# PEER selection for head pairs, one-hot factors of 16 tokens, and the order of POOL's and SyncE's queues

## The chip, the cores and the metric

The kernel runs on one core of one Trainium2 chip. The metric is the device time of one execution in microseconds (us), the median of several runs. The core has five engines that work through queues of their own and wait for each other by semaphores: TensorE (PE; its weight loads are listed as PEld), VectorE (DVE), ScalarE (ACT), GpSimd (POOL) and SyncE (SP), which issues most of the DMAs.

## The reference

Two transformer blocks work on 512 tokens of width 1024. The first is an attention and convolution block with a feed-forward part; the second is a mixer and, as its last step, a mixture of 16384 small experts (PEER). Only this last step is touched:

```python
def peer(h, w_q, sub_keys, expert_u, expert_v):
    q = jnp.einsum('bsd,dq->bsq', h, w_q).reshape(b, s_len, PEER_HEADS, 2, PEER_HALF)
    scores = jnp.einsum('bshpc,hpnc->bshpn', q, sub_keys).astype(jnp.float32)
    top_s, top_i = lax.top_k(scores, PEER_TOPK)
    cand_s = (top_s[..., 0, :, None] + top_s[..., 1, None, :]).reshape(...)
    cand_i = (top_i[..., 0, :, None] * PEER_NKEYS + top_i[..., 1, None, :]).reshape(...)
    best_s, best_pos = lax.top_k(cand_s, PEER_TOPK)
    best_i = jnp.take_along_axis(cand_i, best_pos, axis=-1)
    gate = jax.nn.softmax(best_s, axis=-1)
    ...
        u = jnp.take(expert_u, ib, axis=0)
        act = jax.nn.gelu(jnp.einsum('td,tkd->tk', xb, u), approximate=False)
        vv = jnp.take(expert_v, ib, axis=0)
        return jnp.einsum('tk,tkd->td', (gb * act).astype(h.dtype), vv)
```

There are 8 heads, 128 keys on each of two sides, and 16 experts chosen per head and token, so 128 experts of 128 x 128 for each token.

## The kernel before

The first 1290 us are the first block and the mixer, and then comes `peer`. Of its 512 tokens 384 (`TD`) take a dense path: the activations of all 128 chunks of 128 experts are computed for all of these tokens, and multiplied by a matrix of gates that is zero where an expert was not chosen. The last 128 tokens take the row path: the rows of `expert_u` and `expert_v` that they need are gathered by POOL's indirect DMAs (`r_row`, line 1145), 128 of each, and summed on VectorE.

**Weights.** A load brings 128 x 2048 f32 numbers into `wraw` (SyncE's queue, two buffers). ACT casts them to the leading part `whi` (line 142). The rest, `wlo`, is made by VectorE in one instruction (line 144) or by POOL in four slices of 128 x 512 (line 148). Each product on PE is three matmuls: `whi` with the leading part of the input, `whi` with its rest, and `wlo` with its leading part (lines 153 to 155).

**ahead.** This generator computes the activations of the first 48 expert chunks (`NS`) ahead of time: 24 loads of `expert_u`, two chunks each, 24 matmuls of 128 x 384 a chunk into `pa`, in four steps a chunk, 192 steps in all. For its first 13 loads `wlo` comes from POOL, for the others from VectorE. At a chunk's end ACT applies the gelu (`ex_a`, line 109) and SyncE stores it to `act_dram` (line 1115). The steps are called from `select` (8 for each of heads 0 to 6 and 40 for head 7, `AH`) and from `spread` (16, `LAST`, are held back for after it), and they are what PE does beside the selection.

**select.** It runs over the 8 heads. PE makes the queries of the next head and the scores of this one with the keys (`pb`), ACT copies the scores to `tk_s`, and VectorE finds the 16 best of each side with their indices (`top16`, lines 1184 to 1189: `tk_v`, `tk_i`). POOL adds pairs of them to 112 candidates per token in two instructions (`tk_c`, line 1250). VectorE finds the 16 best of these and their positions (`pk_b`, `tk_p`). The positions are turned into the two key indices of each chosen expert: `ranks` (lines 1197 to 1204), and then for each side a cast (1258), a compare with 0 to 15 (1260), a product with the indices (1263) and a sum over 16 places (1264), into `pk_i` and `pk_j`. At the end VectorE and ACT make the softmax of `pk_b`.

**Between.** `row_places` makes the addresses `r_at` of the row path on VectorE. POOL then issues the first six gathers of `row_experts`, at the line `next(rows)`.

**spread.** It makes the gate matrix for the 384 tokens. For each of three blocks of 128 tokens PE transposes `pk_i`, `pk_j` and `pk_b` (line 1293, `pb<-cst,pk_i`), and ACT copies them to `oh_t` and `oh_g`. Then for each group of 8 tokens VectorE makes four one-hot factors of 128 x 1024 f16: `oh_i` and `oh_j` by comparison (1309, 1311), and `oh_h` and `oh_l`, the factor of `oh_j` with the leading part of the gate and with its rest (1313, 1315), in three buffers each. PE multiplies them, 16 matmuls a group, four tokens to a PSUM bank (`pc`, `pd`, `pb` in turn; lines 1321 and 1322), ACT scales each bank into `oh_s` (1324), and SyncE stores `oh_s` once per 32 tokens to `gate_dram` (1330). Steps of `ahead` lie between the banks.

**experts.** `x_rows` loads the eight `xc` tiles of the residual (1092), PE transposes them in 40 instructions (1100), and ACT copies the results to `y` (1101). Then for each chunk `ex_a` is loaded back (1368), the gates `ex_g` too (1377; for the first chunk in twelve pieces), VectorE multiplies them to `ex_w` (1379), ACT casts it to `hew` (1383), VectorE makes the rest (`lew`, 1384), and PE multiplies them with the chunk of `expert_v` into `pp` (1416, 1417, 1420).

The order on each engine comes from a scheduler that works on the program's order and on dependencies; a tile that takes over the memory of a pool closed before waits for the readers of the old tiles.

## Time and profile before

| what | us |
|---|---|
| median of three runs | 2579.02 |
| lowest and highest of them | 2578.01, 2582.98 |
| the profiled execution, its time | 2575.19 |
| its span in the trace | 2573.4 |
| PE busy | 2489.6 (97%) |
| DVE busy | 1898.0 (74%) |
| ACT busy | 1100.5 (43%) |
| POOL busy | 617.4 (24%) |

The profile is of one execution. Its times count from the start of the span. A row of the timeline gives the start of an instruction, how long it lasted, its engine, line and tiles, and in brackets how long the engine had been idle before it and what ended that idle time. A wait for several things is put down to the one that came last. The granted clock is the mean of TensorE's clock as a share of full speed. A matmul's duration is longer than its distance from the next, since matmuls are pipelined.

### The profile page before, as it was taken

What the parts mean: (1) busy time and instruction counts of PE and PEld (TensorE: products, weight loads), DVE (VectorE), ACT (ScalarE), POOL (GpSimd) and SP (SyncE); (2) the same over time, 40 slices, a digit from 0 to 9 for tenths busy, and PEclk for the clock granted to TensorE, in tenths of its full rate; (3) what the DMA queues carried; (4) which work ended last, traced back from release to release, by engine and by line L of the source; (5) the groups of instructions that cost most, each with busy time, mean ns of one, the idle gap of its engine ahead of it and who ended that gap; (6) DMA issues with size and microseconds to landing.
All of it is one profiled execution on the core that took longest, in us unless ns stands there. A gap on an engine that the chain in (4) does not pass through costs nothing.

```text
span 2573.4 us, 33226 instructions
## 1 busy us (share of the span) xinstructions
PE 2489.6 (97%) x12637; PEld 2118.3 (82%) x12637; DVE 1898.0 (74%) x3238; ACT 1100.5 (43%) x1479; POOL 617.4 (24%) x510
## 2 busy tenths in 40 slices
PE   8999999999999999999999979989999999999999
PEld 6887877877888878777788967868889999999998
DVE  5558777745555567887789989847767777888887
ACT  4226555633222247657643248733333333333332
POOL 0001110111001101101054420001135555555552
PEclk9999999999999999999999989989999999999999
DMA  5352222444444331134333357689879999999995
GB/s 194 128 203 95 101 86 99 170 150 142 161 164 147 131 119 67 58 105 142 131 121 109 119 183 275 266 274 348 298 262 328 326 332 328 328 333 331 331 332 192
DMA packets 172313, 515.04 MB, mean 200 GB/s; under 512 B 13396, under 2 KB 78308, under 8 KB 146296
## 3 DMA queue, kind: packets, MB, share of 16 engines
q1 hardware_dynamic: 133960, 376.52, 41.7%
q0 software_dynamic: 37040, 135.35, 14.6%
q8 instruction: 99, 1.62, 0.2%
q10 hardware_dynamic: 1152, 1.05, 0.1%
q14 instruction: 62, 0.51, 0.1%
HBM read 461.47 MB, written 51.38 MB: 199 GB/s over the span
## 4 chain that ended last, share of the span: by engine, by line
PE 76%; DVE 14%; ACT 5%; issue 2%; DMA 2%; POOL 1%; SPq 0%; DVEq 0%; ACTq 0%; POOLq 0%
PE pa L155 12%; PE pa L153 11%; PE pa L154 11%; PE pp L1417 7%; PE pp L1416 7%; PE pp L1420 7%; PE pu L153 4%; PE pu L155 4%; PE pu L154 4%; ACT whi L142 1%; DVE wlo L144 1%; DVE tk_rest L1187 1%; PE pb L588 1%; PE pc L608 1%; DMA mg_a<-g_dram 1%
## 5 line engine op out<-in xcount | busy, mean ns | idle before, releaser
L142 ACT CAST whi<-wraw 128x2048 fp32r<-128x2048 f32 x229 | 437.7, 1911 | 573.0 <-PE pa L154 295.7
L144 DVE TENSOR_TENSOR wlo<-wraw,whi 128x2048 fp32r<-128x2048 f32 x210 | 492.8, 2346 | 139.0 <-ACT whi L142 134.3
L155 PE MATMUL pa<-hh,wlo 128*128 128x512 f32 (+1 forms) x1360 | 521.8, 385 | 19.8 <-POOL wlo L148 17.2
L153 PE MATMUL pa<-hh,whi 128*128 128x512 f32 (+1 forms) x1360 | 526.4, 387 | 14.9 <-ACT hh L228 10.8
L154 PE MATMUL pa<-lh,whi 128*128 128x512 f32 (+1 forms) x1360 | 523.1, 385 | 0.0
L155 PEld LDWEIGHTS pa<-hh,wlo 128*128 128x128 f32 x1360 | 257.7, 190 | 65.0 <-POOL wlo L148 18.9
L153 PEld LDWEIGHTS pa<-hh,whi 128*128 128x128 f32 x1360 | 258.0, 190 | 61.9 <-ACT hh L228 11.3
L1416 PE MATMUL pp<-whi,hew 128*128 128x512 f32 x768 | 300.1, 392 | 6.4 <-ACT hew L1383 6.4
L1417 PE MATMUL pp<-wlo,hew 128*128 128x512 f32 x768 | 300.6, 392 | 1.6 <-DVE wlo L144 1.6
L1145 POOL DMA_INDIRECT r_row<-in_u_rows,r_at x128 | 186.0, 1453 | 479.5 <-DVE r_w L1166 447.3
L154 PEld LDWEIGHTS pa<-lh,whi 128*128 128x128 f32 x1360 | 258.0, 190 | 44.2 <-issue 6.5
L1420 PE MATMUL pp<-whi,lew 128*128 128x512 f32 x768 | 237.6, 391 | 0.0
L1145 POOL DMA_INDIRECT r_row<-in_expert_v,r_at x128 | 194.9, 1522 | 177.1 <-DVE r_big L1174 139.5
L153 PE MATMUL pu<-hh,whi 128*128 128x384 f32 x640 | 217.0, 339 | 0.0
L155 PE MATMUL pu<-hh,wlo 128*128 128x384 f32 x640 | 216.7, 339 | 0.0
L154 PE MATMUL pu<-lh,whi 128*128 128x384 f32 x640 | 216.3, 338 | 0.0
L1416 PEld LDWEIGHTS pp<-whi,hew 128*128 128x128 f32 x768 | 144.6, 188 | 35.7 <-ACT hew L1383 6.6
L1417 PEld LDWEIGHTS pp<-wlo,hew 128*128 128x128 f32 x768 | 144.4, 188 | 30.4 <-DVE wlo L144 2.5
L1420 PEld LDWEIGHTS pp<-whi,lew 128*128 128x128 f32 x768 | 144.5, 188 | 30.4
L1174 DVE SCALAR_TENSOR_TENSOR r_big<-r_row,r_w,r_big 128x1024 f32<-128x1024 f32 x127 | 162.9, 1283 | 3.0
L1383 ACT CAST hew<-ex_w 128x384 fp32r<-128x384 f32 x128 | 65.6, 513 | 228.3 <-DVE ex_w L1379 151.3
L1166 DVE CUSTOM_DVE_ANT_0 r_row<-r_row,r_big 128x1024 f32<-128x1024 f32 x128 | 151.4, 1220 | 0.0
(436 smaller groups left out, 4552.5 us busy)
## 6 DMA issues: line engine op xcount, KB each, us to landing
wraw<-in_expert_u SPq DMA_DIRECT2D x64, 1024.0 KB, 7.2
wraw<-in_expert_v SPq DMA_DIRECT2D x64, 1024.0 KB, 7.6
wraw<-in_w_in SPq DMA_DIRECT2D x37, 1024.0 KB, 4.8
ada_w<-in_w_ada SPq DMA_DIRECT2D x24, 1024.0 KB, 4.8
gate_dram<-oh_s SPq DMA_DIRECT2D x12, 2048.0 KB, 6.9
ex_g<-gate_dram SPq DMA_DIRECT2D x31, 768.0 KB, 9.9
wraw<-in_w_up SPq DMA_DIRECT2D x16, 1024.0 KB, 5.9
wraw<-in_w_down SPq DMA_DIRECT2D x16, 1024.0 KB, 4.8
```

The costliest lines, as they stand in the source:

```text
L142: nc.scalar.copy(hi, raw)
L144: nc.vector.tensor_sub(lo, raw, hi.bitcast(F32))
L153: mm(out, wh, xh, start=start, stop=False)
L154: mm(out, wh, xl, start=False, stop=False)
L155: return mm(out, wl, xh, start=False, stop=stop)
L1145: self.nc.gpsimd.indirect_dma_start(t, None, src, at)
L1166: later(nc.vector.tensor_tensor_reduce(row, row, h, 1.0, 0.0, op0=ALU.mult, op1=ALU.add, accum_out=w[:, k:k + 1]))
L1174: later(nc.vector.scalar_tensor_tensor(acc, row, w[:, k:k + 1], acc, op0=ALU.mult, op1=ALU.add))
L1383: nc.scalar.copy(hi, w)
L1416: mm(sums[b][half], hi, v[0][:, c, hc], start=n == 0, stop=False)
L1417: mm(sums[b][half], hi, v[1][:, c, hc], start=False, stop=False)
L1420: mm(sums[b][half], lo, v[0][:, c, hc], start=False, stop=n == P - 1)
```

## The change

- **Places.** `places` works for two heads at once, after the odd one. The ranks are 128 wide, and there is one compare and one product of 128 x 4096 f16. The sum over 16 is a tree: additions of 256 x 8, 256 x 4 and 256 x 2 elements in f16, and four small ones into `pk_i` and `pk_j`. The indices `tk_i` and positions `tk_p` of two heads lie in one tile each.
- **Candidates.** Those of heads 6 and 7 are added on VectorE, the others on POOL as before.
- **First gathers.** The first six gathers are no longer issued before `spread` but in it, ahead of its second block of 128 tokens.
- **Spread.** A group is 16 tokens (`G`), so the one-hot factors are 128 x 2048, with two buffers each. A group fills four PSUM banks. `oh_g` and `oh_w` have one buffer.
- **experts.** The pools of `ex_a`, `ex_g` and the others (`et`, `ew`) are opened before `x_rows`, so that the `xc` tiles no longer share their memory with them.

```diff
@@ -25,6 +25,7 @@
 TB = 32
+G = 16
 NS = 48
@@ -1073,8 +1074,7 @@
                 rows = self.row_experts(rp, gp, rows)
-                next(rows)
-                self.spread(kp, Ix, Jx, gate, g_dram, ahead)
+                self.spread(kp, Ix, Jx, gate, g_dram, ahead, rows)
                 for _ in ahead:
@@ -1191,18 +1191,42 @@
         nc = self.nc
-        p4 = tp.tile([P, 64], U32, name="tk_u4", bufs=2)
-        p2 = tp.tile([P, 64], U32, name="tk_u2", bufs=2)
-        c = pos.rearrange("p t r -> p (t r)")
+        n = 128
+        p4 = tp.tile([P, n], U32, name="tk_u4", bufs=1)
+        p2 = tp.tile([P, n], U32, name="tk_u2", bufs=1)
+        c = pos.rearrange("p h t r -> p (h t r)")
         nc.vector.tensor_single_scalar(p4, c, 4, op=ALU.logical_shift_right)
         nc.vector.tensor_single_scalar(p2, c, 2, op=ALU.logical_shift_right)
-        a = tp.tile([P, 64], F32, name="tk_ra", bufs=2)
-        b = tp.tile([P, 64], F32, name="tk_rb", bufs=2)
+        ab = tp.tile([P, 2, n], F32, name="tk_r", bufs=1)
+        a, b = ab[:, 0], ab[:, 1]
         nc.vector.scalar_tensor_tensor(a, p2, -12.0, p4, op0=ALU.add, op1=ALU.max)
...
         nc.vector.tensor_sub(b, c, b)
-        return a, b
+        return ab
+
+    def places(self, tp, idx, pos, iota, h, dsts):
+
+        nc = self.nc
+        idf = tp.tile([P, 2, 2, 4, 16], F16, name="tk_f", bufs=1)
+        nc.vector.tensor_copy(idf, idx)
+        pf = tp.tile([P, 256, 2], F16, name="tk_pf", bufs=1)
+        nc.vector.tensor_copy(pf, self.ranks(tp, pos).rearrange("p s r -> p (s r)").unsqueeze(2).to_broadcast([P, 256, 2]))
+        eq = tp.tile([P, 256, 16], F16, name="tk_e", bufs=1)
+        nc.vector.tensor_tensor(eq.rearrange("p r (a b) -> p r a b", b=2), pf.unsqueeze(2).to_broadcast([P, 256, 8, 2]),
+                                iota, op=ALU.is_equal)
+        e = eq.rearrange("p (s r) n -> p s r n", r=16)
+        idf = idf.rearrange("p s h t n -> p (s h t) n").unsqueeze(2).to_broadcast([P, 16, 16, 16])
+        nc.vector.tensor_mul(e, e, idf)
+        n = 8
+        while n > 1:
+            nc.vector.tensor_add(eq[:, :, 0:n], eq[:, :, 0:n], eq[:, :, n:2 * n])
+            n //= 2
+        e = eq.rearrange("p (s h t r) n -> p s h t r n", s=2, h=2, t=4)
+        for s, dst in enumerate(dsts):
+            d = dst[:, :, 16 * h:16 * h + 32].rearrange("p t (h r) -> p h t r", h=2)
+            for i in range(2):
+                nc.vector.tensor_add(d[:, i], e[:, s, i, :, :, 0], e[:, s, i, :, :, 1])

@@ -1213,7 +1237,7 @@
             nc.vector.tensor_copy(iota, self.iota[:, 0:16])
-            iota = iota.rearrange("p (a b) -> p a b", b=2).unsqueeze(1).to_broadcast([P, 64, 8, 2])
+            iota = iota.rearrange("p (a b) -> p a b", b=2).unsqueeze(1).to_broadcast([P, 256, 8, 2])
             keys = tp.tile([P, 16 * P], F32, name="keys")
@@ -1229,8 +1253,10 @@
                 vals = tp.tile([P, 4, 2, 16], F32, name="tk_v", bufs=2)
-                idx = tp.tile([P, 4, 2, 16], U32, name="tk_i", bufs=2)
-                pos = tp.tile([P, 4, 16], U32, name="tk_p", bufs=2)
+                if h % 2 == 0:
+                    idx2 = tp.tile([P, 2, 2, 4, 16], U32, name="tk_i", bufs=2)
+                    pos2 = tp.tile([P, 2, 4, 16], U32, name="tk_p", bufs=2)
+                idx, pos = idx2[:, :, h % 2], pos2[:, h % 2]
                 for half in range(2):
@@ -1241,27 +1267,18 @@
                         tb, p = 2 * half + i // 2, i % 2
-                        self.top16(tp, sc[:, i * P:(i + 1) * P], vals[:, tb, p, :], idx[:, tb, p, :], P)
+                        self.top16(tp, sc[:, i * P:(i + 1) * P], vals[:, tb, p, :], idx[:, p, tb, :], P)
                     steps(AH[h] // 4)
...
                     o = cand[:, :, at:at + (a1 - a0) * n].rearrange("p t (a b) -> p t a b", b=n)
-                    nc.gpsimd.tensor_add(o, vals[:, :, 0, a0:a1].unsqueeze(3).to_broadcast(s),
+                    (nc.gpsimd if h < 6 else nc.vector).tensor_add(o, vals[:, :, 0, a0:a1].unsqueeze(3).to_broadcast(s),
                                          vals[:, :, 1, 0:n].unsqueeze(2).to_broadcast(s))
...
                     self.top16(tp, cand[:, tb, :], best[:, tb, h, :], pos[:, tb, :], NC)
-                idf = tp.tile([P, 4, 2, 16], F16, name="tk_f", bufs=2)
-                nc.vector.tensor_copy(idf, idx)
-                for p, src, dst in zip(range(2), self.ranks(tp, pos), (Ix, Jx)):
-                    pf = tp.tile([P, 64, 2], F16, name="tk_pf", bufs=2)
-                    nc.vector.tensor_copy(pf, src.unsqueeze(2).to_broadcast([P, 64, 2]))
-                    eq = tp.tile([P, 64, 16], F16, name="tk_e", bufs=3)
-                    nc.vector.tensor_tensor(eq.rearrange("p r (a b) -> p r a b", b=2),
-                                            pf.unsqueeze(2).to_broadcast([P, 64, 8, 2]), iota, op=ALU.is_equal)
-                    e = eq.rearrange("p (t r) n -> p t r n", t=4)
-                    nc.vector.tensor_mul(e, e, idf[:, :, p, :].unsqueeze(2).to_broadcast([P, 4, 16, 16]))
-                    nc.vector.tensor_reduce(dst[:, :, 16 * h:16 * h + 16], e, axis=AX.X, op=ALU.add)
+                if h % 2:
+                    self.places(tp, idx2, pos2, iota, h - 1, (Ix, Jx))
                 steps(AH[h] - AH[h] // 4 * 2)
@@ -1284,10 +1301,12 @@
             nc.vector.tensor_copy(iota16, self.iota)
-            iota = two(iota16).unsqueeze(1).to_broadcast([P, 8, P // 2, 2])
+            iota = two(iota16).unsqueeze(1).to_broadcast([P, G, P // 2, 2])
             after = self.last
-            left, groups, nb = NS * 4 - sum(AH) - LAST, TD // 8, 0
+            left, nb = NS * 4 - sum(AH) - LAST, 0
             for tb in range((TD + P - 1) // P):
+                if tb == 1:
+                    next(fetch)
                 pt = self.psum("b", 2)
@@ -1295,25 +1314,25 @@
                 nc.scalar.copy(ij.rearrange("p a b c -> p (a b) c"), pt[:, :2 * P].unsqueeze(2).to_broadcast([P, 2 * P, 2]))
-                gs = tp.tile([P, P], F32, name="oh_g")
+                gs = tp.tile([P, P], F32, name="oh_g", bufs=1)
                 nc.scalar.activation(gs, pt[:, 2 * P:3 * P], AF.Copy, scale=2.0 ** 14)
-                gh = tp.tile([P, 2, P, 2], F16, name="oh_w")
+                gh = tp.tile([P, 2, P, 2], F16, name="oh_w", bufs=1)
                 gs = gs.unsqueeze(2).to_broadcast([P, P, 2])
...
                 nc.vector.tensor_sub(gh[:, 1], gs, gh[:, 0])
-                for t0 in range(0, min(P, TD - tb * P), 8):
+                for t0 in range(0, min(P, TD - tb * P), G):
                     if t0 % TB == 0:
                         stage = tp.tile([P, P, TB], F32, name="oh_s")
-                    bc = lambda t: t[:, t0:t0 + 8].unsqueeze(2).to_broadcast([P, 8, P // 2, 2])
-                    oi = tp.tile([P, 8, P], F16, name="oh_i", bufs=3)
+                    bc = lambda t: t[:, t0:t0 + G].unsqueeze(2).to_broadcast([P, G, P // 2, 2])
+                    oi = tp.tile([P, G, P], F16, name="oh_i", bufs=2)
                     nc.vector.tensor_tensor(rows(oi), iota, bc(ij[:, 0]), op=ALU.is_equal)
-                    oj = tp.tile([P, 8, P], F16, name="oh_j", bufs=3)
+                    oj = tp.tile([P, G, P], F16, name="oh_j", bufs=2)
                     nc.vector.tensor_tensor(rows(oj), iota, bc(ij[:, 1]), op=ALU.is_equal)
-                    oh = tp.tile([P, 8, P], F16, name="oh_h", bufs=3)
+                    oh = tp.tile([P, G, P], F16, name="oh_h", bufs=2)
                     nc.vector.tensor_mul(rows(oh), rows(oj), bc(gh[:, 0]))
-                    ol = tp.tile([P, 8, P], F16, name="oh_l", bufs=3)
+                    ol = tp.tile([P, G, P], F16, name="oh_l", bufs=2)
                     nc.vector.tensor_mul(rows(ol), rows(oj), bc(gh[:, 1]))
-                    for f in range(2):
+                    for f in range(G // 4):
                         pg = self.psum("cdb"[nb % 3])
@@ -1323,10 +1342,10 @@
                                              pg.rearrange("p (t i) -> p t i", t=4), AF.Copy, scale=2.0 ** -14)
-                        n = (tb * P + t0) // 8 * 2 + f
-                        for _ in range((n + 1) * left // (2 * groups) - n * left // (2 * groups)):
+                        n = (tb * P + t0) // 4 + f
+                        for _ in range((n + 1) * left // (TD // 4) - n * left // (TD // 4)):
                             next(ahead, None)
-                    if (t0 + 8) % TB == 0:
+                    if (t0 + G) % TB == 0:
                         nc.sync.dma_start(g_dram[(tb * P + t0) // TB], stage)
@@ -1350,10 +1369,10 @@
         yp = es.enter_context(self.pool("ey"))
+        tp = es.enter_context(self.pool("et", bufs=2))
+        wp = es.enter_context(self.pool("ew", bufs=LEAD + 2))
         xs = self.x_rows(yp, x_dram)
         self.xs, self.g2 = xs, xs[4]
-        tp = es.enter_context(self.pool("et", bufs=2))
-        wp = es.enter_context(self.pool("ew", bufs=LEAD + 2))
         nb = TD // P
```

**POOL's queue at the end of the selection.** Before (`wlo` are the slices for `ahead`, `tk_c` the candidates of heads 6 and 7, `r_row` the gathers of the row path):

```order
L148 TENSOR_TENSOR wlo<-wraw,whi 128x512 x8
L1250 TENSOR_TENSOR tk_c<-tk_v 128x4x48
L1250 TENSOR_TENSOR tk_c<-tk_v 128x4x64
L148 TENSOR_TENSOR wlo<-wraw,whi 128x512 x8
L1250 TENSOR_TENSOR tk_c<-tk_v 128x4x48
L1250 TENSOR_TENSOR tk_c<-tk_v 128x4x64
L148 TENSOR_TENSOR wlo<-wraw,whi 128x512 x5
L1145 DMA r_row<-in_u_rows,r_at 128x1024 x6
L148 TENSOR_TENSOR wlo<-wraw,whi 128x512 x3
```

After (the first two rows are the candidates of head 5):

```order
L1276 TENSOR_TENSOR tk_c<-tk_v 128x4x48
L1276 TENSOR_TENSOR tk_c<-tk_v 128x4x64
L149 TENSOR_TENSOR wlo<-wraw,whi 128x512 x24
L1145 DMA r_row<-in_u_rows,r_at 128x1024 x128
L1145 DMA r_row<-in_expert_v,r_at 128x1024 x128
```

The candidates of heads 6 and 7 are gone from this queue, and all 24 slices now stand ahead of the first gather.

**SyncE's queue from the end of the spread to the first expert chunk.** Before (`xc` are the residual tiles that are transposed, `act_dram` the stores of the last chunks of `ahead`, `ex_a` and `ex_g` the loads for the experts):

```order
L1115 DMA act_dram<-ex_a 128x384
L1092 DMA xc_15245<-x_dram 128x512
L1092 DMA xc_15247<-x_dram 128x512
L1092 DMA xc_15249<-x_dram 128x512
L1092 DMA xc_15251<-x_dram 128x512
L1092 DMA xc_15253<-x_dram 128x512
L1115 DMA act_dram<-ex_a 128x384
L1092 DMA xc_15255<-x_dram 128x512
L1368 DMA ex_a<-act_dram 128x384
L1377 DMA ex_g<-gate_dram 128x128 x12
L1368 DMA ex_a<-act_dram 128x384 x2
```

After:

```order
L1092 DMA xc_14953<-x_dram 128x512
L1092 DMA xc_14955<-x_dram 128x512
L1115 DMA act_dram<-ex_a 128x384
L1092 DMA xc_14957<-x_dram 128x512
L1092 DMA xc_14959<-x_dram 128x512
L1092 DMA xc_14961<-x_dram 128x512
L1387 DMA ex_a<-act_dram 128x384
L1396 DMA ex_g<-gate_dram 128x128
L1115 DMA act_dram<-ex_a 128x384
L1396 DMA ex_g<-gate_dram 128x128 x11
L1387 DMA ex_a<-act_dram 128x384 x2
```

The eight `xc` loads stand closer together, and the loads `ex_a` and `ex_g` around the last store; before, `ex_a` and the first `ex_g` carry a wait for PE, and after they carry none.

**VectorE's queue in the spread.** Before, the second to fourth group (`oh_i`, `oh_j`, `oh_h`, `oh_l` are the one-hot factors):

```order
L1309 TENSOR_TENSOR oh_i<-oh_n,oh_t 128x1024
L1313 TENSOR_TENSOR oh_h<-oh_j,oh_w 128x1024
L1315 TENSOR_TENSOR oh_l<-oh_j,oh_w 128x1024
L1311 TENSOR_TENSOR oh_j<-oh_n,oh_t 128x1024
L1309 TENSOR_TENSOR oh_i<-oh_n,oh_t 128x1024
L1313 TENSOR_TENSOR oh_h<-oh_j,oh_w 128x1024
L1315 TENSOR_TENSOR oh_l<-oh_j,oh_w 128x1024
L1311 TENSOR_TENSOR oh_j<-oh_n,oh_t 128x1024
```

After, from the first group on:

```order
L1328 TENSOR_TENSOR oh_i<-oh_n,oh_t 128x2048
L1321 CAST oh_w<-oh_g 128x256
L1330 TENSOR_TENSOR oh_j<-oh_n,oh_t 128x2048
L1322 TENSOR_TENSOR oh_w<-oh_g,oh_w 128x256
L1332 TENSOR_TENSOR oh_h<-oh_j,oh_w 128x2048
L1334 TENSOR_TENSOR oh_l<-oh_j,oh_w 128x2048
L1328 TENSOR_TENSOR oh_i<-oh_n,oh_t 128x2048
L1330 TENSOR_TENSOR oh_j<-oh_n,oh_t 128x2048
L1328 TENSOR_TENSOR oh_i<-oh_n,oh_t 128x2048
L1332 TENSOR_TENSOR oh_h<-oh_j,oh_w 128x2048
L1334 TENSOR_TENSOR oh_l<-oh_j,oh_w 128x2048
L1330 TENSOR_TENSOR oh_j<-oh_n,oh_t 128x2048 x2
```

Each row now covers 16 tokens, and the `oh_i` of the next group stands ahead of the `oh_h` of this one as it did, but in one of two buffers and not of three.

## Rows read from the trace of the kernel before

**Rows 1.** The page, part 4: share of the span of the chain that ended last.

```profile
PE 76%; DVE 14%; ACT 5%; issue 2%; DMA 2%; POOL 1%; SPq 0%; DVEq 0%; ACTq 0%; POOLq 0%
```

**Rows 2.** Waits of PE, whole span: what, total us, times, longest us.

```profile
PE pa L155 <- POOL wlo L148: 17.2, 3, 9.5
...
PE pp L1416 <- ACT hew L1383: 6.4, 1, 6.4
```

**Rows 3.** Slices: length, busy us of PE, PEld, DVE, ACT, POOL; granted clock; DMA share; GB/s.

```profile
1460.00:1470.00 10.00, 8.39 (x45) 7.33 (x44) 9.90 (x67) 3.33 (x5) 6.35 (x7) 1.00 0.00 1
...
1480.00:1490.00 10.00, 3.84 (x22) 3.51 (x20) 9.90 (x64) 2.67 (x3) 2.39 (x4) 0.86 0.05 19
1490.00:1500.00 10.00, 9.99 (x46) 9.96 (x47) 9.86 (x39) 0.24 (x1) 4.91 (x4) 0.80 0.51 152
1500.00:1510.00 10.00, 2.02 (x11) 1.42 (x9) 6.10 (x9) 6.58 (x8) 6.70 (x5) 0.88 0.56 191
1510.00:1520.00 10.00, 7.27 (x28) 7.18 (x29) 7.04 (x4) 2.48 (x4) 4.80 (x5) 0.61 1.02 396
```

**Rows 4.** Timeline of POOL, 1486 to 1503: start, us, instruction, idle before it.

```profile
1487.02 0.51 POOL L1250 TENSOR_TENSOR tk_c<-tk_v 128x192 f32<-128x192 f32 x1 [12.28 <-DVE tk_v L1188]
...
1488.70 6.21 POOL L148 TENSOR_TENSOR wlo<-wraw,whi 128x512 fp32r<-128x512 f32 x5
1502.09 3.01 POOL L1145 DMA_INDIRECT r_row<-in_u_rows,r_at  x1 [7.17 <-DVE oh_n L1286]
```

**Rows 5.** Timeline of PE, 1490 to 1513.

```profile
1490.01 0.69 PE L155 MATMUL pa<-hh,wlo 128*128 128x384 f32 x1 [6.18 <-POOL wlo L148]
...
1501.53 0.33 PE L1293 MATMUL pb<-cst,pk_j 128*128 128x128 f32 x1 [1.26 <-DVE pk_j L1264]
...
1512.73 0.69 PE L155 MATMUL pa<-hh,wlo 128*128 128x384 f32 x1 [9.45 <-POOL wlo L148]
```

**Rows 6.** Groups of VectorE, 1305 to 1502: busy us, mean ns, idle before.

```profile
L1263 DVE TENSOR_TENSOR tk_e<-tk_e,tk_f 128x1024 f16<-128x1024 f16 x16 | 13.8, 866 | 0.2
...
L1264 DVE TENSOR_REDUCE pk_j<-tk_e 128x64 f32<-128x1024 f16 x8 | 9.7, 1217 | 0.2
...
L1202 DVE TENSOR_SCALAR tk_rb<-tk_ra 128x64 f32<-128x64 f32 x8 | 5.3, 667 | 0.2
```

**Rows 7.** Timeline of VectorE, 1494.9 to 1496.

```profile
1494.99 0.68 DVE L1270 TENSOR_TENSOR pk_b<-pk_b,pk_t 128x512 f32<-128x512 f32 x1
...
1495.83 0.19 DVE L1202 TENSOR_SCALAR tk_rb<-tk_ra 128x64 f32<-128x64 f32 x1
```

**Rows 8.** Groups of all engines in the spread, 1519 to 1665.

```profile
L1324 ACT ACTIVATE oh_s<-pc 128x512 f32<-128x512 f32 x32 | 36.4, 1138 | 5.6 <-PE pc L1322 5.3 <-ACT oh_s L1324 0.3
...
L1309 DVE TENSOR_TENSOR oh_i<-oh_n,oh_t 128x1024 f16<-128x1024 f16 x48 | 32.8, 683 | 5.7 <-ACT oh_t L1297 3.1 <-PE pd L1322 2.1 <-PE pb L1322 0.5
...
L144 DVE TENSOR_TENSOR wlo<-wraw,whi 128x2048 fp32r<-128x2048 f32 x9 | 20.5, 2280 | 0.0
```

**Rows 9.** Stretches: spread, long products after it, start of experts, experts.

```profile
1524.40:1664.90 140.50, 129.97 (x1207) 112.65 (x1205) 132.25 (x197) 116.73 (x126) 0.00 (x0) 0.99 0.64 249
1664.90:1680.10 15.20, 15.20 (x89) 15.20 (x87) 2.29 (x1) 4.92 (x6) 0.00 (x0) 1.00 0.72 274
1680.10:1698.80 18.70, 9.27 (x42) 6.41 (x40) 0.56 (x1) 6.66 (x12) 0.00 (x0) 0.73 0.46 140
1720.00:2555.00 835.00, 834.96 (x4093) 746.73 (x4092) 657.51 (x722) 288.77 (x302) 370.01 (x247) 1.00 0.90 318
```

**Rows 10.** Timeline of SyncE at the start of the experts.

```profile
1690.71 5.54 SPq L1377 DMA_DIRECT2D ex_g<-gate_dram  x12
```

**Rows 11.** Timeline of VectorE there.

```profile
1697.70 0.56 DVE L1379 TENSOR_TENSOR ex_w<-ex_a,ex_g 128x384 f32<-128x384 f32 x1 [26.92 <-DMA ex_g<-gate_dram]
```

**Rows 12.** Timeline of PE there.

```profile
1686.40 4.70 PE L1100 MATMUL pu<-cst,xc 128*128 128x128 f32 x20 [0.25 <-ACT y L1101]
...
1698.86 0.80 PE L1416 MATMUL pp<-whi,hew 128*128 128x512 f32 x1 [6.38 <-ACT hew L1383]
```

More of the change, by code (lines that the diff above doesn't have):

```diff
@@ L1276, in select, with spread @@
         return Ix, Jx, gate.rearrange("p a h r -> p a (h r)")
-    def spread(self, kp, Ix, Jx, gate, g_dram, ahead):
+    def spread(self, kp, Ix, Jx, gate, g_dram, ahead, fetch):
         nc = self.nc
```

## Prediction

> **What bounds the kernel now.** I read the page first, then the waits of TensorE, then TensorE's busy time in slices of 10 us, then the instructions around the two slices that stand out. The chain that ended last lies 76% on PE [rows 1], so a microsecond counts when PE loses it. The reader should look for places where PE stops in the last part of the program (the selection, the spread and the start of the experts), since only that part is touched. The waits name them: 17.2 us in three waits for a `wlo` made on POOL and one wait of 6.4 us for `hew` [rows 2]. The slices put them in time: 8.39 us of work at 1460 to 1470, 3.84 at 1480 to 1490, 2.02 at 1500 to 1510, and 7.27 at 1510 to 1520 [rows 3].
>
> **Transition from selection to spread.** PE stops three times for the same reason: POOL works its queue in order, and what stands ahead of the next `wlo` waits for VectorE. Before the first product at 1490.01 PE was idle 6.18 us for `wlo` [rows 5]; POOL had itself waited 12.28 us for `tk_v` before the candidates at 1487.02 and only then, at 1488.70, took up the `wlo` [rows 4]. Before 1512.73 PE was idle 9.45 us [rows 5]; POOL had waited 7.17 us for `oh_n` and then issued six gathers from 1502.09 on, with the last three `wlo` slices behind them [rows 4]. The third wait of the 17.2 is what is left, 17.2 - 9.5 - 6.2 = 1.5 us, and lies in the slice at 1460 (10 - 8.39 = 1.6). Both long stops are followed by a stretch at the lower of the two clocks (1.2 against 2.4 GHz; the granted clock is 0.80 and 0.61 in the slices behind them [rows 3]). At full clock a product of this chain comes every 15.2 / 86 = 0.177 us (the stretch after the spread, where 86 long products, of the row's 89, run without a stop [rows 9]). The slice from 1490 spent 9.99 us on 46 products and the slice from 1510 7.27 us on 28 [rows 3], so the low clock cost 9.99 - 8.14 = 1.9 and 7.27 - 4.96 = 2.3 us. One more wait, 1.26 us for `pk_j` at 1501.53 [rows 5], belongs here.
>
> The change takes both obstacles out of POOL's queue: the candidates of heads 6 and 7 go to VectorE, and the gathers go behind all 24 slices. POOL then runs at PE's pace: one load of weights is four slices of 6.21 / 5 = 1.24 us [rows 4] and feeds 48 products of 8.5 us. So all of 1.6 + 6.2 + 1.9 + 1.3 + 9.5 + 2.3 = **22.8 us** can go, if VectorE is ready when PE comes. PE would reach the transposes of `pk_i` at 1501.5 - 1.3 - 1.6 - 6.2 - 1.9 = 1490.5.
>
> VectorE's side: per head the two one-hot compares, two products and two sums cost 2 x (0.87 + 0.87 + 1.22) = 5.9 us if a compare costs what a product does, with nine small instructions of up to 0.67 on top [rows 6], so about 18 us for two heads. For the pair I take one rate for all f16 work with two inputs. An f32 subtraction costs 0.68 us at 512 elements [rows 7] and 2.28 at 2048 [rows 8]; an f16 one of 1024 costs 0.68 [rows 8], as f32 of half the size. So f16 of 2048 should cost about 1.22 and of 4096 about 2.3. Compare 2.3, product 2.3, tree 1.2 + 0.7 + 0.4, four last adds 0.9, ranks and casts 2.3: 10 us; with the tree at f32's rate 12, with the small ones stretched as now up to 15. I take 12, so 6 us saved per pair. The candidates cost VectorE about 0.8 us a head (256 and 192 f32 elements). VectorE ends `pk_j` now at 1501.5; the last pair's places replace 9 us of head 6 and 9 of head 7 by 12 at the end, and the earlier pairs save too, so 1501.5 - 6 - 6 + 1.6 = 1491 if only one earlier pair's saving reaches the end, 1486 if more. That is level with PE's arrival; I take 22.5 of it and keep 0 to 5 us as a loss.
>
> Here the trace shows that VectorE and POOL disturb each other: the `tk_rb` operation costs 0.19 us by itself and 0.67 on average over the selection [rows 6, 7]. The Trainium skill ("SBUF — State Buffer", section "SBUF: two separate sides") says that VectorE's instructions in its two-port modes or with two inputs in SBUF and GpSimd's share a port pair under a lock held for a whole instruction, so that the later one waits. By that rule the new 2.3 us instructions would hold POOL up, and POOL's slices the small ones. The stretched row agrees with it; its price is the second rival below.
>
> **Spread.** Now 192 one-hot instructions of 0.68 us [rows 8] come every 0.6 us (132.25 us busy less 20.5 for nine `wlo` and some 3 for small ones, over 184 [rows 8, 9]): 115 us. After: 96 of 1.22, every 1.14: 109.5. VectorE is busy 132 of 140.5 us here and PE 130 [rows 9], and neither is alone the bound; ACT is busy 117. ACT's 96 evacuations of 1.14 us [rows 8] stay the same, and so do PE's 768 small products. What changes on PE is their grain: 32 at once, then 15 to 20 of the long ones, with three PSUM banks for four evacuations per group, and two buffers of 16 tokens instead of three of 8. In VectorE's order the `oh_i` of the next group stands before the `oh_h` and `oh_l` of this one, as it did, but it must now wait until PE has ended the group two before, not three. Working the steady order through by hand with these durations gives 5.4 us per 16 tokens where few long products lie between and 5.8 to 6.2 where many do; now it is 140.5 / 24 = 5.85. The six gathers inside cost nothing: POOL is idle for the whole spread [rows 9] and their data are used after it. From first one-hot product to the end of the long ones (155.7 us now, with 86 long products behind the last one-hot; 94 after) I take a gain of **2 us**; bounds: all of VectorE's 5.5 plus its idle time, 7, on one side, and 8 us lost on the other.
>
> **Start of the experts.** Now PE ends the long products at 1680.1 and starts the first expert product at 1698.86, 18.8 us later, at granted clock 0.73 [rows 9, 12]. `ex_a` and the twelve `ex_g` loads can't be issued before the transposes have read the `xc` tiles, since they lie in the same memory: they start at 1690.71 and take 5.54 us to issue; `ex_w` starts at 1697.70 and `hew` at once behind it [rows 10 to 12]. With their own memory they follow `act_dram` directly: the last store is issued after the last gelu, for which I allow 0.9 us, eleven loads take 11 x 0.46 = 5.1, and landing takes the same 1697.70 - (1690.71 + 5.54) = 1.45, so `ex_w` could start at end + 7.5. Then the 40 transposes with their 10 copies, which stay ahead of the first product on both engines, become the bound: 20 transposes now take 4.70 us [rows 12], so 40 take 9.4, and a last copy and `hew`, half a microsecond each, follow. First product at end + 10.4, gain 8.4. A low clock such as the one that cost 1.9 and 2.3 us above follows this wait too (the first product lasts 0.80 us [rows 12]) and may go or not. I take **9.5**, with half of it; bounds 7 to 11. Everything behind, 835 us in which PE never stops [rows 9], is untouched.
>
> **Sum.** 22.5 + 2 + 9.5 = 34. The profiled execution took 2575.2, so 2541; the runs' median is 2579.0, 3.8 above it, so **2545**. With the losses above (5, 10 and 2.5) and gains (0, 5 and 1.5) the forecast's own range is 2537 to 2553.
>
> **Rivals.**
> - *Coupled buffers.* With two buffers, VectorE and PE wait for each other in each group and the spread loses 8 to 12 us: 2555. For it: VectorE and PE both lie above 92% in the spread [rows 9], with no other slack. Against: only 24 hand-overs instead of 48.
> - *The wait changes its name.* VectorE is late with the last pair, since nine small instructions are stretched by 0.5 us each behind POOL (4.3 us), or the tree is slow: PE waits 4 to 9 us at `pk_i`, and may drop to the low clock: 2551 to 2554. This is what the lock of the Trainium skill ("SBUF — State Buffer", section "SBUF: two separate sides") would do; the stretched row speaks for it.
> - *VectorE alone bounds the spread*, and its whole saving arrives: 2538.
> - *Slower than before.* The cycle of a group becomes serial: four one-hot instructions 4.55, then 32 small products 1.8, then the last evacuation 0.9, 7.3 us per 16 tokens instead of 5.85. That costs 24 x 1.4 = 34 us and eats the whole gain; from 7.3 us per group it decides, and at 7.6 the time is 2586. For it: the two buffers. Against: VectorE's order starts the next group's `oh_i` and `oh_j` before the last is used.
> - *It does not do what it says.* Next in line behind POOL's `wlo` are the loads of `wraw` (two buffers) and ACT's casts, which may be late as well; with half the transition and a bad spread the net is near zero: 2575 to 2584.
>
> **How the numbers follow.** Forecast 0.56, coupled buffers 0.14, changed name 0.12, VectorE alone 0.08, slower 0.06, nothing 0.04. The range takes in the first four: 2534 to 2560, and leaves out about 0.18. This kernel's measurements tell 0.2%, 5 us, from no change. Faster 0.90, same 0.04, slower 0.06.
>
> **What would show it.** Right: no wait of PE for POOL's `wlo`, first one-hot product near 1502 (now 1524.4), spread of 138 to 141 us, first expert product 9 to 10.5 us after the long ones, `ex_g` issued before the transposes. Wrong: a wait of PE for `pk_i` or `pk_j` over 4 us, one-hot instructions of 2048 elements well over 1.25 us, PE waits for `oh_h` or `oh_i` that sum to over 10 us, or a low clock in the spread.

## The result and the profile after

The changed kernel takes 2547.05 us (median of four runs, 2545.76 to 2549.65) where the kernel before takes 2579.2. The ratio is 0.9874, with a 95% interval of 0.9857 to 0.9891. The forecast was 2545, with a range of 2534 to 2560. The profiled execution took 2545.76, with a span of 2544.0 (before 2573.4): 29.4 us less.

The waits of PE from the first one-hot product (1500.9) to the end of the long products (1660.9) are these (what, total us, times, longest us):

```profile
PE pd L1340 <- ACT oh_s L1343: 8.9, 15, 1.3
PE pc L1340 <- ACT oh_s L1343: 6.1, 14, 0.7
PE pa L154 <- ACT ex_a L110: 1.0, 1, 1.0
PE pb L1340 <- DVE oh_h L1332: 0.7, 1, 0.7
```

The wait for POOL's `wlo`, 17.2 us in [rows 2], is gone from the whole profile. The waits for `oh_s` are now 29, of 15.0 us: PE wants to write a PSUM bank that ACT has not scaled yet. Before there were six, of 5.7 us:

```profile
PE pd L1321 <- ACT oh_s L1324: 3.9, 4, 1.1
PE pc L1321 <- ACT oh_s L1324: 1.8, 2, 1.0
```

The slices over the old gaps, in the columns of [rows 3]:

```profile
1470.00:1480.00 10.00, 10.00 (x58) 10.00 (x57) 9.79 (x46) 2.87 (x4) 5.03 (x4) 1.00 0.49 154
1480.00:1490.00 10.00, 9.65 (x56) 9.20 (x55) 9.72 (x14) 4.31 (x4) 0.33 (x1) 1.00 0.35 136
1490.00:1500.00 10.00, 9.51 (x55) 9.19 (x54) 9.12 (x11) 6.51 (x9) 8.78 (x5) 1.00 0.73 256
```

In the slices from 1480 and 1490 PE works 9.65 and 9.51 us at a granted clock of 1.00; before, it worked 3.84 us in the first and ran at a granted clock of 0.80 in the second [rows 3]. POOL and PE at the transition (start, us, instruction, idle before):

```profile
1473.43 5.03 POOL L149 TENSOR_TENSOR wlo<-wraw,whi 128x512 fp32r<-128x512 f32 x4 [3.44 <-ACT whi L143]
1489.67 3.01 POOL L1145 DMA_INDIRECT r_row<-in_u_rows,r_at  x1 [11.21 <-DVE oh_n L1303]
```

```profile
1488.83 0.30 PE L1312 MATMUL pb<-cst,pk_i 128*128 128x128 f32 x1 [0.35 <-DVE pk_i L1229]
1500.88 0.23 PE L1340 MATMUL pc<-oh_i,oh_h 128*128 128x128 f16 x1
1669.83 0.50 PE L1435 MATMUL pp<-whi,hew 128*128 128x512 f32 x1 [1.41 <-ACT hew L1402]
1680.02 1.66 PE L1435 MATMUL pp<-whi,hew 128*128 128x512 f32 x6 [1.63 <-ACT whi L143]
```

POOL ends its last slice 11 us before the gathers, and PE waits 0.35 us for `pk_i`: VectorE and PE arrive together. The stretches of [rows 9], now spread, long products behind it, start of experts:

```profile
1500.90:1644.20 143.30, 126.46 (x1197) 114.65 (x1196) 127.24 (x106) 111.97 (x125) 0.69 (x1) 1.00 0.68 266
1644.20:1660.90 16.70, 16.70 (x99) 16.66 (x97) 2.29 (x1) 5.99 (x8) 0.00 (x0) 1.00 0.75 274
1660.90:1669.80 8.90, 6.16 (x41) 4.16 (x39) 0.60 (x2) 6.50 (x12) 0.00 (x0) 1.00 0.70 215
```

So the time went as follows:

| stage | before | after | gain | forecast |
|---|---|---|---|---|
| to the first one-hot product | 1524.4 | 1500.9 | 23.5 | 22.5 |
| from there to the end of the long products | 155.7 | 160.0 | -4.3 | 2 |
| from there to the first expert product | 18.7 | 8.95 | 9.8 | 9.5 |
| from there to the end | 874.5 | 874.2 | 0.3 | 0 |

Of the 23.5 us, 1.0 lies ahead of the selection, where nothing was changed: VectorE's first instruction of the selection, the copy `tk_n`, starts that much earlier in the profiled execution (before, then after):

```profile
1301.18 1.28 DVE L1215 CAST tk_n<-iota 128x16 f16<-128x16 f32 x1
1300.16 1.28 DVE L1239 CAST tk_n<-iota 128x16 f16<-128x16 f32 x1
```

From `tk_n` to the first one-hot product the selection took 223.2 us and now takes 200.7, which is 22.5 us less.

### The profile page after: what moved, and what is told of

Same layout as the page of the kernel before. It is cut to its first block, busy times and chain, and to the rows that moved or that the text cites. A ratio compares the mean times of both kernels' runs of the same rounds, so it can differ in the third digit from the quotient of the medians.

```text
span 2544.0 us, 33077 instructions
## 1 busy us (share of the span) xinstructions
PE 2478.2 (97%) x12637; PEld 2114.3 (83%) x12637; DVE 1868.4 (73%) x3094; ACT 1098.0 (43%) x1479; POOL 627.2 (25%) x506
## 5 line engine op out<-in xcount | busy, mean ns | idle before, releaser
L1145 POOL DMA_INDIRECT r_row<-in_u_rows,r_at x128 | 190.2, 1486 | 467.2 <-DVE r_w L1166 430.6
## 6 DMA issues: line engine op xcount, KB each, us to landing
ex_g<-gate_dram SPq DMA_DIRECT2D x31, 768.0 KB, 11.3
```

What stands on the lines that cost most here:

```text
L1145: self.nc.gpsimd.indirect_dma_start(t, None, src, at)
```

## Experiments

All runs change the changed kernel; medians of four runs. `tk_n` starts anywhere from 1300.1 to 1303.8 in these runs, though nothing ahead of it differs, and totals scatter by 2 to 3 us. So a stage is read from its own length, and the selection from `tk_n` on: 200.6 to 200.9 us in the runs that leave it alone (199.1 with groups of 8 in the scheduler's order).

### What each part is worth: one part undone

**The first gathers back before the spread.**

```diff
+                next(rows)
                 self.spread(kp, Ix, Jx, gate, g_dram, ahead, rows)
...
-                if tb == 1:
-                    next(fetch)
```

> The changed kernel with the first six gathers issued before the spread again. If they cost what the prediction took, the idle of 9.5 us and the low clock of 2.3 us behind it, the time is 2547 + 8 to 12 = 2555 to 2559, with a wait of TensorE for POOL's wlo of 7 to 10 us. If POOL, free of the candidates of heads 6 and 7, has made all its slices before the gathers come up, nothing changes: 2546 to 2549.

2548.74 us, no wait of PE for POOL's `wlo`; selection and spread as in the changed kernel (200.9 and 160.1 us). POOL had ended its slices at 1480.0 and had nothing else to do when the gathers came up, 11.3 us later. The gathers' move is worth nothing beside the other parts. The run doesn't bring back the old queue, though: no slice stands behind the gathers here, where three did before, so what that order would cost beside the faster places was not tried.

**Candidates of heads 6 and 7 back on POOL.**

```diff
-                    (nc.gpsimd if h < 6 else nc.vector).tensor_add(o, ...
+                    nc.gpsimd.tensor_add(o, ...
```

> The changed kernel with the candidates of heads 6 and 7 back on POOL. The run with the gathers moved back showed that these cost nothing by themselves, so by elimination the candidates should be what freed POOL: then TensorE's waits for POOL's wlo come back (1.6 and 6.2 us and 1.9 at the low clock), 2554 to 2558. Rival: with the faster places VectorE delivers tk_v early enough, POOL is held up by less than the lead it has, and the time is 2546 to 2550; then it was the places that removed the waits.

2551.99 us, 4.9 more, by neither mechanism as I had put it: POOL's `wlo` isn't waited for, although POOL waits for `tk_v` again. POOL's timeline, and PE's one new wait:

```profile
1470.70 0.51 POOL L1276 TENSOR_TENSOR tk_c<-tk_v 128x192 f32<-128x192 f32 x1 [2.93 <-DVE tk_v L1188]
...
1477.84 5.48 POOL L149 TENSOR_TENSOR wlo<-wraw,whi 128x512 fp32r<-128x512 f32 x4 [0.36 <-ACT whi L143]
```

```profile
PE pb L1312 <- DVE pk_i L1229: 2.4, 1, 2.4
```

The candidates of head 7 are made at 1470.7 and not at 1487.0 [rows 4], in time for the last slices. What is lost is time of VectorE in the hand-over: from `tk_n`, `pk_j` ends 2.0 us later than in the changed kernel, and PE waits 2.4 us for `pk_i`. The selection is 2.0 us longer (202.7); the rest of the 4.9 us lies outside it, and the intervals of the two kernels overlap (0.9873 to 0.9906 here), so 2.0 us is what this part is shown to be worth.

**Places per head again** (`ranks` and the loop behind the candidates as before the change).

```diff
-                if h % 2:
-                    self.places(tp, idx2, pos2, iota, h - 1, (Ix, Jx))
+                for p, src, dst in zip(range(2), self.ranks(tp, pos), (Ix, Jx)):
+                    ...
+                    nc.vector.tensor_reduce(dst[:, :, 16 * h:16 * h + 16], e, axis=AX.X, op=ALU.add)
```

> The changed kernel with the places made per head, as before; candidates of heads 6 and 7 stay on VectorE. If VectorE is behind all through the selection, its saving of some 6 us per pair adds up: pk_j ends near 1501 as before instead of 1489.05, TensorE waits 10 to 13 us for pk_i or pk_j and then runs a stretch at the low clock: 2558 to 2562. If only the last pair's saving counts: pk_j near 1495, 2552 to 2555. If the places do not matter: 2546 to 2549.

2563.02 us, 16.0 more. Waits of PE, and two slices:

```profile
PE pb L1295 <- DVE pk_i L1264: 11.6, 1, 11.6
PE pb L1295 <- DVE pk_j L1264: 2.0, 1, 2.0
```

```profile
1490.00:1500.00 10.00, 2.01 (x12) 1.69 (x10) 9.90 (x66) 3.57 (x3) 0.00 (x0) 0.73 0.28 107
1500.00:1510.00 10.00, 4.35 (x14) 4.09 (x15) 9.86 (x17) 1.91 (x2) 3.05 (x2) 0.50 0.07 8
```

POOL is idle, VectorE is busy 9.9 of 10 us, and the gap is back under another name, with a granted clock of 0.73 and 0.50. The selection takes 217.5 us, 16.8 more than in the changed kernel and only 5.8 less than before the change. That is more than the 6 us that the prediction put on one pair, so the earlier pairs' savings reach the end too. VectorE waits only 7.8 us in the whole selection here and before the change, 6.8 of them ahead of its first `top16`: it was the bound of the selection from the start, and POOL's waits were how its lateness reached PE.

**The `xc` tiles back in the memory of `ex_a` and `ex_g`.**

```diff
-        tp = es.enter_context(self.pool("et", bufs=2))
-        wp = es.enter_context(self.pool("ew", bufs=LEAD + 2))
         xs = self.x_rows(yp, x_dram)
+        tp = es.enter_context(self.pool("et", bufs=2))
+        wp = es.enter_context(self.pool("ew", bufs=LEAD + 2))
```

> The changed kernel with the xc tiles in the memory of ex_a and ex_g again. By the prediction's sum the first expert product comes 18 to 19 us after the long products and not 8.95, and the time is 2547 + 9 to 10.5 = 2556 to 2558. If part of the gain came from the loads that now stand closer together in SyncE's queue, or if a wait for weights of expert_v behind it takes part of it back, the loss is 5 to 8 us.

2554.8 us, 7.7 more. The first expert product comes 14.6 us after the long ones: 5.6 of the 9.8 us are the wait that the shared memory made. The other 4.1 came with the `xc` loads, which stand closer together in either kernel (five in 2.29 us, then three): PE's waits for them are 1.0 us here and were 2.9 before, and 12 transposes take 1.99 us as in the changed kernel. That is put down to the loads by elimination, not tried alone.

### Why the spread became longer

The theory was *groups of 16 with two buffers cost it*; the rivals were the three PSUM banks and PE's order.

**Groups of 8 with three buffers, all else as changed.**

```diff
-G = 16
+G = 8
...
-                    oi = tp.tile([P, G, P], F16, name="oh_i", bufs=2)
+                    oi = tp.tile([P, G, P], F16, name="oh_i", bufs=3)
```

> The changed kernel with groups of 8 tokens and three buffers each in the spread, as before; all else as changed. The changed kernel takes 2547.05 us; from its first one-hot product (1500.9) to the end of the long products (1660.9) it needs 160.0 us, where the kernel before needed 155.7. If the groups of 16 are what costs these 4.3 us: 155 to 157 us in that stretch and a time of 2542 to 2544. If the stretch is longer for another reason (it starts earlier, with less of the long work done, or the gathers run beside it): 159 to 161 us and 2546 to 2548.

2543.75 us, and 155.9 us for the stretch. So groups of 16 with two buffers cost the 4.3 us. PE's waits for `oh_s` are 5.5 us again. The total gains 3.3 us: the first one-hot product comes 1.7 us earlier after `tk_n`, the start of the experts takes 13.1 us and not 8.95 (PE waits 3.3 us for `xc` loads, which stand apart again), and the rest is 2.3 us shorter.

**Three buffers for `oh_i`, one for `oh_j`.**

```diff
-                    oi = tp.tile([P, G, P], F16, name="oh_i", bufs=2)
+                    oi = tp.tile([P, G, P], F16, name="oh_i", bufs=3)
...
-                    oj = tp.tile([P, G, P], F16, name="oh_j", bufs=2)
+                    oj = tp.tile([P, G, P], F16, name="oh_j", bufs=1)
```

> The changed kernel with three buffers for oh_i and one for oh_j (which only VectorE reads), in the same memory. If two buffers couple VectorE and TensorE: VectorE's waits before oh_i for TensorE (11.1 us in the changed kernel) fall below 4, the spread gains 4 to 8 us, and the time is 2539 to 2543. If the banks are the limit, VectorE only moves its wait to oh_h, and the time stays at 2546 to 2548.

2549.01 us, but the stretch is 154.6 us, 5.4 less than in the changed kernel and as short as with groups of 8. VectorE's waits before `oh_i` for PE, 11.1 us in the changed kernel, fell to 2.7. In the changed kernel they were:

```profile
DVE oh_i L1328 <- PE pc L1341: 6.8, 4, 3.7
DVE oh_i L1328 <- PE pd L1341: 3.6, 2, 3.3
DVE oh_i L1328 <- PE pb L1341: 0.7, 1, 0.7
```

The total doesn't show the gain because the start of the experts takes it back, 17.9 us and not 8.95. The scheduler now puts all eight `xc` loads behind the last two stores to `act_dram`, and PE stands idle after its last long product (PE, then SyncE):

```profile
1656.63 0.34 PE L156 MATMUL pa<-hh,wlo 128*128 128x384 f32 x1
1660.95 0.30 PE L1100 MATMUL pu<-cst,xc 128*128 128x128 f32 x1 [3.98 <-DMA xc<-x_dram]
1674.72 0.50 PE L1435 MATMUL pp<-whi,hew 128*128 128x512 f32 x1 [1.08 <-ACT hew L1402]
```

```profile
1653.33 4.56 SPq L1115 DMA_DIRECT2D act_dram<-ex_a  x2
1657.99 3.70 SPq L1092 DMA_DIRECT2D xc<-x_dram  x8
```

So the two buffers of `oh_i` were the limit in the stretch: with a third, groups of 16 lose nothing there. The scheduler's order changed with the edit, and what the buffer is worth in a fixed order was not tried.

**Four banks in turn.**

```diff
-                        pg = self.psum("cdb"[nb % 3])
+                        pg = self.psum("cdbb"[nb % 4])
```

> The changed kernel with four PSUM banks in turn for the one-hot products (both buffers of pb each time) where it has three. If TensorE's burst of four banks is held up by ACT's evacuations (29 waits of TensorE for oh_s, 15.0 us, where the kernel before had 6 and 5.7): these waits fall below 5 us, the spread gains 4 to 8 us, and the time is 2539 to 2543. If the buffers or VectorE are the limit, the waits change their name to oh_h or oh_l and the time stays at 2546 to 2548.

2551.55 us, and 160.3 us. The waits for `oh_s` are 10.3 us, now mostly at `pb`, and two more, 2.6 us together, stand before the transposes. A fourth bank is no help either.

**Four banks with groups of 8.** (Both edits together.)

> Groups of 8 with three buffers and four PSUM banks; all else as changed. If the banks limit groups of 8 as well: 1 to 4 us less than groups of 8 with three banks. If only bursts of 16 tokens need a fourth bank, the two agree within 1 us. If VectorE is the bound of groups of 8 (192 instructions every 0.6 us), they agree too, and four banks with groups of 16 are the faster by up to 6 us.

2544.03 us, 154.2 us: 1.7 us less in the stretch than with three banks, and no wait for `oh_s`, but no gain in the total.

**PE's order fixed.** From the first to the last one-hot product PE has about 117 us of work, an estimate: 421 long products at 0.177 us and 768 one-hot ones that start 0.056 us apart. So of 143 us it loses 26. In the changed kernel it mostly runs 28 or 29 one-hot products in a row, then 2 to 25 long ones, 3 or 4 one-hot ones, and 5 or 6 long ones (so it does with the third `oh_i` buffer, too). This edit makes long and one-hot products follow each other bank by bank (`behind` orders two instructions of one engine; `pace` is the last one-hot product):

```diff
+                    for _ in range(10):
+                        next(ahead, None)
...
-                            nc.tensor.matmul(o, oh[:, i, :], oi[:, i, :], start=True, stop=False)
-                            nc.tensor.matmul(o, ol[:, i, :], oi[:, i, :], start=False, stop=True)
+                            mm = nc.tensor.matmul(o, oh[:, i, :], oi[:, i, :], start=True, stop=False)
+                            self.behind(mm, self.last)
+                            mm = nc.tensor.matmul(o, ol[:, i, :], oi[:, i, :], start=False, stop=True)
+                        self.pace = mm.ins.name
```

> The changed kernel with TensorE's order in the spread fixed: ten steps of the long products ahead of the first one-hot product, and then bank by bank, 8 one-hot products and mostly 6 long ones in turn (the changed kernel runs 24 to 32 one-hot products in a row, with 2 to 25 long ones between). Groups of 16, two buffers and three banks stay. If the burst on TensorE costs the 4.3 us (a fourth bank can't help it, since ACT needs 3.7 us for four banks in any case): TensorE's waits for oh_s fall from 15.0 to below 5 us, the stretch from first one-hot product to the end of the long ones falls from 160.0 to 150 to 155, and the time to 2538 to 2542. If groups of 16 with two buffers are the limit whatever the order: TensorE waits for oh_h or oh_l instead, and the stretch stays at 158 to 162.

2547.18 us and 158.3 us for the stretch: no gain in the total, but the waits for `oh_s` are gone, and VectorE's waits before `oh_i` for PE are 0.6 us. VectorE and PE wait elsewhere:

```profile
DVE wlo L145 <- ACT whi L143: 9.5, 1, 9.5
DVE oh_i L1335 <- ACT oh_t L1320: 9.5, 2, 4.8
PE pd L1347 <- ACT whi L143: 5.1, 1, 5.1
PE pb L1347 <- DVE oh_h L1339: 4.7, 1, 4.7
```

The two waits for `oh_t` stand at the block ends: the transposes of the next 128 tokens come behind the last group. (VectorE's 9.5 us for `whi` lie behind the last factor.) PE's two waits follow from them: at both, the `oh_h` of the new block ends just before PE goes on. Behind them the granted clock is low, in the slices from 1550 and from 1600:

```profile
1550.00:1560.00 10.00, 8.19 (x64) 7.38 (x65) 9.37 (x9) 5.56 (x7) 0.00 (x0) 0.67 0.52 187
1600.00:1610.00 10.00, 9.13 (x74) 8.18 (x75) 9.99 (x9) 5.90 (x8) 0.00 (x0) 0.78 0.44 156
```

> The same fixed order with groups of 8 and three buffers. If order alone matters, it is like the paced groups of 16, or up to 5 us slower because VectorE needs 115 us for 192 one-hot instructions and not 109 for 96. If the size of a group matters by itself, it is 3 to 5 us faster than the paced groups of 16. A third case: the fixed order is worse than the planned one for both, since a late factor now also stops the long products: 2546 to 2552.

The same order with groups of 8: 2541.18 us, 154.0 us.

**The same order, and the transposes 32 tokens earlier.**

```diff
+                    if t0 == P - 32 and tb + 1 < blocks:
+                        ready = prep(tb + 1)
                     if t0 % TB == 0:
```

> Groups of 16 in the fixed order, and the transposes of the next 128 tokens (with ACT's copies to oh_t and oh_g) 32 tokens earlier. In the fixed order without this TensorE's waits for oh_s were gone, but VectorE waited 9.5 us for oh_t at the two block ends, and the time stayed at 2547.18. If that boundary is what kept the gain away: VectorE's wait for oh_t below 2 us, first one-hot product to the end of the long ones 149 to 152 us instead of 158.3, and 2538 to 2541. If groups of 16 lose elsewhere (TensorE's waits for oh_h and oh_l with only two groups of lead): 155 to 159 us and 2544 to 2548.

2534.41 us (2533.41 to 2537.75; ratio to the kernel before 0.9823, 0.9807 to 0.984): the lowest of all, 12.6 us below the changed kernel. 146.1 us for the stretch.

> Groups of 8, three buffers, in the fixed order, with the same early transposes. Here VectorE did not wait for oh_t, so little should change against 2541.18: 2539 to 2542. Against the paced groups of 16 with early transposes it tells what the size of a group is worth when the order is the same: VectorE needs 115 us for its factors here and 109 there.

Groups of 8: 2538.62 us, 151.2 us. The spread in both, first with groups of 16, then of 8:

```profile
1504.50:1632.50 128.00, 122.81 (x1188) 110.51 (x1189) 126.58 (x106) 115.63 (x125) 0.73 (x1) 1.00 0.75 293
```

```profile
1500.70:1633.80 133.10, 125.29 (x1190) 110.95 (x1189) 133.10 (x200) 118.55 (x125) 0.53 (x1) 1.00 0.73 283
```

VectorE is busy 126.58 of 128.00 and 133.10 of 133.10 us: it is the bound now, and only here does the saving of the larger groups arrive, 5.1 us of the 5.5 reckoned. The order alone gave 1.7 us (158.3 against 160.0), order and early transposes together 13.9. Early transposes without the order weren't tried, nor with a third `oh_i` buffer.

## Why the prediction was right, and where it was not

**Transition: 22.5 us measured in the selection, 22.5 forecast.** The size holds, the mechanism only in part. The prediction ascribed 9.5 + 2.3 us to the gathers ahead of `wlo` and most of the rest to the candidates on POOL. Undone one at a time, the gathers cost nothing that can be told from the scatter and the candidates 2.0 us, while the places per head cost 16.8 (gathers and candidates undone together were not tried). The step that failed is the one that read POOL's queue as the cause: POOL's 12.28 us for `tk_v` and 7.17 for `oh_n` [rows 4] were both waits for VectorE, so what ended the idle time of PE was one station further back. The prediction had this as a condition ("if VectorE is ready when PE comes") and the pair's price of 12 us was good. The last pair in the changed kernel runs 1476.6 to 1489.1, 12.5 us:

```profile
1476.61 0.69 DVE L1198 TENSOR_SCALAR tk_u<-tk_p 128x128 uint32<-128x128 uint32 x1
1477.22 1.33 DVE L1199 TENSOR_SCALAR tk_u<-tk_p 128x128 uint32<-128x128 uint32 x1
...
1480.76 2.29 DVE L1216 TENSOR_TENSOR tk_e<-tk_pf,tk_n 128x4096 f16<-128x4096 f16 x1
1483.08 2.29 DVE L1220 TENSOR_TENSOR tk_e<-tk_e,tk_f 128x4096 f16<-128x4096 f16 x1
1485.41 2.78 DVE L1223 TENSOR_TENSOR tk_e<-tk_e 128x2048 f16<-128x2048 f16 x3
```

Compare and product are 2.29 us each, as put at 2.3. The rival that had instructions stretched behind POOL came to little in this pair: two rows, of 0.69 and 1.33 us, while POOL still ran (0.34 and 0.21 in the first pair, when it did not). PE was 0.35 us early. In the first three pairs the rival's other half came true, a slow tree, though too early for PE to wait at `pk_i`. POOL makes slices beside it there; its three additions take 5.6 to 5.7 us and not 2.78, and in the first pair four of POOL's slices take 7.94 us and not 5.03:

```profile
1351.13 5.67 DVE L1223 TENSOR_TENSOR tk_e<-tk_e 128x2048 f16<-128x2048 f16 x3
1350.02 7.94 POOL L149 TENSOR_TENSOR wlo<-wraw,whi 128x512 fp32r<-128x512 f32 x4 [5.49 <-ACT whi L143]
```

The sums that the tree replaced took 1.22 us on average over the selection [rows 6] and 1.21 and 1.22 in the last head, so they were not stretched. The tree's stretch is some 8.6 us of VectorE's time in the stage that it bounds (an estimate, three times 2.9); no run removed it.

**Spread: -4.3 measured, +2 forecast.** The step that failed is the replay of the steady groups by hand, which let VectorE wait for the group two before and still gave a gain. The term for VectorE was right (1.22 us an instruction, 24 of each kind). The rival *coupled buffers* named the cause that the runs bear out, at twice its size: it laid 8 to 12 us to the two buffers, and they cost 4.3. VectorE waited 11.1 us for PE before `oh_i`; a third buffer for `oh_i` or groups of 8 took the stretch back to 154.6 and 155.9 us, and a fourth bank did not (160.3). PE's order is the other side of the same tie: the replay spaced the long products evenly (15 to 20 a group), while in the changed kernel they come in lumps of 2 to 25, and a burst of one-hot products stands before a bank that ACT still scales. An even order removes VectorE's wait as the third buffer does, and needs the early transposes to be worth something. Of the signs that the prediction gave, the spread of 138 to 141 us was missed (143.3), but none of those for "wrong" came: they asked for PE's waits at `oh_h` and `oh_i` (0.7 us), and PE waited at `oh_s`.

**Start of the experts: 9.8 measured, 9.5 forecast.** First product 8.95 us after the long ones and not 10.4, since the 40 transposes no longer ran at the low clock (12 in 1.99 us, before 20 in 4.70 [rows 12]). The half of a low clock that was added was not got: the first products run faster now, and a wait of 1.63 us for `whi` of the next weights at 1680.02 takes it back.

**The sum.** That the median lies 2 us from the forecast is in part luck. The profiled execution was forecast at 2541 and took 2545.76; the 3.8 us added for the distance from the profiled execution to the median were 1.3. Two of the prediction's sums don't add up: its losses and gains (17.5 and 6.5 us) give 2538.5 to 2562.5 and not 2537 to 2553, with the spread's gain of up to 12.5 entered as 5 on top of 2, and a cycle of 7.6 us gives some 2589 and not 2586.

**Rivals.** Slower than before did not come near: the group's cycle was 143.3 / 24 = 5.97 us, not 7.3. That VectorE alone bounds the spread became true only with another order.

## What to carry to other kernels

When the engine that is waited for is itself waiting, follow the chain to the one that was never idle: moving work out of POOL's queue alone renamed the gap, and shortening VectorE's work closed it. Larger groups with fewer buffers tie the producer to the consumer; here the saving on the producer arrived only when that tie was loosened and the block boundary prepared ahead. Undo parts one at a time, and read each stage up to the end of its own work: here one part was worth nothing, one cost 4 us, and a buffer that took them back didn't show in the total, because the next stage's loads came late.

## What was not expected of the hardware

The gathers on POOL took longer where VectorE was at work beside them. Before, the five behind the first took 0.93 to 0.99 us each, with VectorE idle for most of the time; in the changed kernel they took 1.04 to 1.95, while VectorE ran `wlo`, small instructions and the one-hot factors:

```profile
1492.98 1.85 POOL L1145 DMA_INDIRECT r_row<-in_u_rows,r_at  x1 [0.31 <-issue]
1495.13 1.38 POOL L1145 DMA_INDIRECT r_row<-in_u_rows,r_at  x1 [0.30 <-issue]
1496.82 1.95 POOL L1145 DMA_INDIRECT r_row<-in_u_rows,r_at  x1 [0.30 <-issue]
```

That agrees only in part with the lock of the Trainium skill ("SBUF — State Buffer", section "SBUF: two separate sides"), by which the later of the two would be held for a whole instruction: the last two gathers, of 1.04 and 1.17 us, had VectorE at work beside them all the time. No run varied it alone, and nothing waited for these gathers.
